# Forget rows in two buffers and masked in place, the last queries earlier, three blocks of the last unit on VectorE

## Chip, cores and metric

The kernel runs on one core of a Trainium2 chip. The metric is the device time of one execution in microseconds (us). The engines are TensorE (PE in the profile, with its weight loads as PEld), VectorE (DVE), ScalarE (ACT), GpSimd (POOL) and SyncE (SP), which here only issues DMA transfers. Every engine works through its own instructions in order. The order on each engine is fixed when the kernel is built: a scheduler takes the instructions as they are written, estimates when each would be ready, and lays out each engine's list; some stretches are pinned to the written order.

## Reference, cut to what matters

One decoder block with two parallel branches over 512 positions and width 1024, in fp32. After an RMS norm one wide projection gives the inputs of both branches.

```python
hN = _rmsnorm(x, norm_g[l])
p = _split_in(hN @ w_in[l])
mq = silu(_causal_dwconv(p["m_q"], ...)); mk = silu(_causal_dwconv(p["m_k"], ...))
mh = _mlstm(mq, mk, p["m_v"], p["m_i"] + b_igate, p["m_f"] + b_fgate)      # 4 heads of 256
mh = _head_layernorm(mh, mh_norm_g[l])
ya = sigmoid(p["m_o"]) * mh * silu(p["m_z"])
yn = _nsa(q_raw, q_rope, kc, vc, ks, vs, kw, vw, gates)                    # 8 heads of 64
yb = yn * silu(p["n_z"])
merged = sigmoid(p["g_a"]) * (ya @ w_branch_a[l]) + sigmoid(p["g_b"]) * (yb @ w_branch_b[l])
x = x + merged @ w_out[l]
return _rmsnorm(x, final_norm_g)
```

In `_mlstm` the scores of a head, q times k, are multiplied by a decay matrix: the exponential of a term of the column position (the input gate minus the running sum of the log forget gate) minus a running maximum, which is a term of the row position, and zero where the column lies after the row. In `_nsa` each query head attends to compressed, selected and windowed keys; the queries of the last two are rotated by position (`_partial_rope`), and each branch's softmax is weighted by a gate.

## The kernel before, in words

All matrices stand as pairs of a rounded high part and the rest (`hTh`/`hTl`, `wh`/`wl` and so on). A product takes three matmuls: high times high, high times low, low times high. The high part is usually made by ACT and the low part by DVE (`split`).

**Start.** `x` comes in four blocks of 128 rows. For each block the mean square is formed on ACT (`square`), a first guess of the reciprocal root by a logarithm and an exponential (`guess`), one Newton step (`newton`, on DVE for blocks 0 and 1, on POOL for 2 and 3; operands of one element per partition), the scaling on DVE (`scaled`), four transposes on PE (`turned`) and the split into `hTh` and `hTl`. In this stretch the engines keep the written order. Meanwhile the small projection's weights are split by POOL, ACT and DVE (`small_hi`, `small_lo`).

**Stream.** The large projection is cut into jobs of 128 columns: a 512 KB weight load on SP (`wr`), the split, 24 matmuls into a PSUM bank of the `pp` ring (L217, L219, L221), and a `post` that reads the bank. Jobs stand in a queue, `stream`, whose loads run two jobs ahead; `stream.step(n)` issues n matmuls of it between other work. The kinds used here:

- `conv_job`: a channel group of the convolution for q or k of the mLSTM branch; its `post` takes an ACT activation, three multiply-adds on DVE, a tanh on ACT, one more DVE product, a split, and a 512 KB store (`qk`).
- `gate_job`: a tanh on ACT and a store (`away`).
- `queries(c)`: two query heads. `rope_a` copies the bank (`rw`), multiplies by the cosines (`ra`), splits the unrotated queries (`rh`, `rl`) and, when the next job begins, moves rows of the copy into `rot` by four small DMAs. `query_heads(c)` multiplies `rot` by the sines, adds, and splits into two `Th` tiles.
- `zpath(c)`: put at the head of the queue when a pair of heads is done.

The queue's order is written by hand: after `queries(1)` come conv, gate, conv, `queries(2)`, conv, gate, conv, gate, conv, `queries(3)`, and then gates and convs in turn.

**Attention units.** 16 units (pair of heads c, head hh, branch b) run in order, with stream matmuls between. While unit i is transposed and multiplied with the values, the scores of unit i + 1 are formed: four row blocks of 128, 256, 384 and 512 columns, each with a fused mask and minimum on DVE, and an exponential on ACT that also gives the row sum. After the fourth one reciprocal of the sums is taken (`st`), and POOL multiplies each block by reciprocal and gate (`P<-P,st,gates`). `ptrans` then transposes four to one blocks on PE into a bank of the `pt` ring (L1020), the result is split into `pth` and `ptl`, and after a lag of three steps multiplied with the values (L1032, L1033). During the units `chores` start copies and sums of weight blocks in DRAM (`wsumv`, `wsumz`, `wsumout`, 1 MB each, issued by SP and POOL).

**Value and gate projections** follow as strips of fewer, summed products, on the same stream. Then the pool `ml` is opened for the **mLSTM heads**. Its tiles have one buffer each unless stated. `fetch_qk(h)` loads q and k of head h (four transfers of 512 KB) and the head's row of running maxima, broadcast to 128 partitions (`gb`, 256 KB, L1376), from DRAM (`decayed`). Four conv jobs run, and more are queued as filler. `decay(h)` makes `Dm`, the decay matrix of head h, in four column blocks of 512, 384, 256 and 128 columns: DVE adds a mask to a copy of the row (`dg`), and ACT takes the exponential of the masked copy for the diagonal 128 columns of each block and of the unmasked `gb` for the rest, seven activations. The head's loop then forms score blocks in two `ps` banks (L170 to L172), DVE multiplies each by its block of `Dm`, in place, and it is split into `Sh` and `Sl`; the value products follow (`num`), their norm (`va`, a power on POOL, some small DVE operations), the products with the gate, `decay(h + 1)`, 30 stream matmuls, and eight transposes (L1510). The output stage ends the kernel.

Of the kernel before, what the change touches and what calls it, by code (L numbers as in the profile page):

```python
# [11 lines left out]
F32 = mybir.dt.float32  # L12
F32R = mybir.dt.float32r
I32 = mybir.dt.int32
AF = mybir.ActivationFunctionType
OP = mybir.AluOpType
AX = mybir.AxisListType.X

T = 512
D = 1024  # L20
NT = T // 128
# [56 lines left out]
def build(  # L78
# [3 lines left out]
    nc = tc.nc  # L82
    ordered = {"act", "dve"}

    class Engine:
# [15 lines left out]
    act, dve, pool = (  # L101
        Engine(e, n) for e, n in ((nc.scalar, "act"), (nc.vector, "dve"), (nc.gpsimd, "pool"))
    )
    A = act.activation
# [170 lines left out]
    gates = pers.tile([128, NT, 24], F32, name="gates")  # L275
    cs = pers.tile([128, NT, 6], F32, name="cs")[:, :, :4]
# [23 lines left out]
    with tc.tile_pool(name="ph0", bufs=2, side="right") as p0, tc.tile_pool(  # L300
        name="small", bufs=1, side="right"
# [16 lines left out]
        bias = sp.tile([128, 32], F32, name="bias")  # L318
# [43 lines left out]
        def newton(tb, e):  # L362
            r, v = rs[tb], vs[tb]
            if e is dve:
                e.scalar_tensor_tensor(v, r, v[:, 0:1], r, OP.mult, OP.mult)
            else:
                e.tensor_tensor(v, r, v, OP.mult)
                e.tensor_tensor(v, r, v, OP.mult)
            e.tensor_scalar(v, v, -0.5, 1.5, OP.mult, OP.add)
            e.tensor_tensor(r, r, v, OP.mult)  # L370

        gp = sp.tile([128, NT, 32], F32, name="gp")
        cols(NKC, lambda ps: blocks(0)(ps))
# [63 lines left out]
        for k in range(7):  # L437
            o = k % 4 * 128
# [139 lines left out]
    def gate_job(n=1):  # L578
        for _ in range(n):
            gate_ab(*gate_jobs.popleft())  # L580
# [25 lines left out]
    def conv_job(n=1):  # L606
        for _ in range(n):
            conv(*conv_jobs.popleft())
# [139 lines left out]
    def queries(c):  # L748
        def post(ps):
            rope_a(ps, ("q", c))  # L750

        cols(NQ + c * 128, post)
# [37 lines left out]
    queries(1)  # L790
    for n in (1, 2, 3):
        conv_job()
        gate_job()
        if n == 1:
            conv_job()
            queries(2)
        elif n == 3:
            conv_job()
            queries(3)
    for _ in range(3):  # L800
        gate_job()
        conv_job()
# [22 lines left out]
    decayed = dram.tile([4, T], F32, name="decayed")  # L825
# [105 lines left out]
    KOFF = [0, 512, 896, 1152]  # L931
# [58 lines left out]
    def score(c, hh, b, qb, pair):  # L990
        kh, kl = KK[c // 2]
        n = (qb + 1) * 128
        tq = heads[c][2][hh][:, qb * 128 : qb * 128 + 128]
        if qb == 0:
            if b == 0:
                pss = PS()
                pe.matmul(pss[:, :256], tq, kh[:, :, :128], start=True, stop=False)
                pe.matmul(pss[:, :256], tq, kl[:, :, :128], start=False, stop=True)
                for i in range(2):
                    softmax_block(c, hh, i, 0, pss[:, i * 128 : i * 128 + 128], *pair[i])  # L1000
            return
        pss = PS()
        pe.matmul(pss[:, :n], tq, kh[:, b, :n], start=True, stop=False)
        pe.matmul(pss[:, :n], tq, kl[:, b, :n], start=False, stop=True)  # L1004
        P, st = pair[b]
        softmax_block(c, hh, b, qb, pss[:, :n], P, st)
        if qb == NT - 1:
            dve.reciprocal(st[:, 2], st[:, 1])
            for j in range(NT):
                pj = P[:, POFF[j] : POFF[j] + (j + 1) * 128]  # L1010
                g = (2 * c + hh) * 3 + 1 + b
                pool.tensor_scalar(
                    pj, pj, st[:, 2, j : j + 1], gates[:, j, g : g + 1], OP.mult, OP.mult
                )

    def ptrans(P, kb):
        n = 512 - kb * 128
# [125 lines left out]
    st = stp.__enter__()  # L1143
# [221 lines left out]
    mp = mlp.__enter__()  # L1365
    cvp.append(mp)
    tiles_of = {}

    def fetch_qk(h):
        for i in range(2):  # L1370
            both = [mp.tile([128, 2, T], F32R, name=f"qk{i}{n}", tag=f"qk{i}{n}") for n in range(2)]
            for n in range(2):
                nc.sync.dma_start(f(both[n]), qk[i, h][:, n])
            tiles_of[i, h] = both
        tiles_of["g", h] = mp.tile([128, T], F32, name="gb", tag="gb")
        nc.sync.dma_start(tiles_of["g", h], decayed[h].partition_broadcast(128))  # L1376

    fetch_qk(0)
    wbv = w_branch_b[0].rearrange("(k p) c -> p k c", p=128)

# [49 lines left out]
    first_of_a(1, PP)  # L1430
    first_of_a(4, PP)

    decays = {}

    def decay(h):
        pgb = tiles_of.pop(("g", h))
        dg = mp.tile([128, T], F32, name="dg", tag="dg")
        dve.tensor_tensor(
            dg.rearrange("p (b t) -> p b t", b=NT), pgb.rearrange("p (b t) -> p b t", b=NT),
            later_only, OP.add,  # L1440
        )
        Dm = mp.tile([128, 1280], F32, name="Dm", tag="Dm")
        for sb in range(NT):
            o, n = KOFF[sb], 512 - sb * 128
            bias = cs[:, sb, h : h + 1]
            A(Dm[:, o : o + 128], dg[:, sb * 128 : sb * 128 + 128], AF.Exp, bias=bias, scale=-1.0)
            if n > 128:
                A(Dm[:, o + 128 : o + n], pgb[:, (sb + 1) * 128 :], AF.Exp, bias=bias, scale=-1.0)
        decays[h] = Dm

    decay(0)
    for h in range(4):
        (qh, ql), (kh, kl) = tiles_of[0, h], tiles_of[1, h]
        vh, vl = vals(h), vals_low(h)
        Dm = decays.pop(h)
        Sh = mp.tile([128, 1280], F32R, name="Sh", tag="Sh")
        Sl = mp.tile([128, 1280], F32R, name="Sl", tag="Sl")
        for sb in range(NT):
            o, n = KOFF[sb], 512 - sb * 128
            pss = PS()  # L1460
            ss = slice(sb * 128, sb * 128 + 128)
            mm3(
                pss[:, :n], lambda k: kh[:, k, ss], lambda k: kl[:, k, ss],
                lambda k: qh[:, k, sb * 128 :], lambda k: ql[:, k, sb * 128 :], range(2),
            )
            dv = Dm[:, o : o + n]
            dve.scalar_tensor_tensor(dv, pss[:, :n], 0.015625, dv, OP.mult, OP.mult)
            split(dv, Sh[:, o : o + n], Sl[:, o : o + n])
            stream.step(6)
        if h < 3:  # L1470
            fetch_qk(h + 1)
        chores.popleft()()
        num = mp.tile([128, NT, 258], F32, name="num", tag="num")
        bs = mp.tile([128, NT, 6], F32, name="bs", tag="bs")
        mv = mp.tile([128, NT, 2], F32, name="mv", tag="mv")
        for tb in range(NT):
            po = PT()
            for sb in range(tb + 1):
                a = KOFF[sb] + (tb - sb) * 128
                lh, ll = Sh[:, a : a + 128], Sl[:, a : a + 128]  # L1480
                pe.matmul(po[:, :258], lh, vh[:, sb, :], start=sb == 0, stop=False)
                pe.matmul(po[:, :256], lh, vl[:, sb, :], start=False, stop=False)
                pe.matmul(po[:, :258], ll, vh[:, sb, :], start=False, stop=sb == tb)
            A(num[:, tb], po[:, :258], AF.Copy)
            dve.bn_stats(bs[:, tb], num[:, tb, 0:256])
            dve.bn_aggr(mv[:, tb], bs[:, tb])
            stream.step(6)
        rho = mp.tile([128, NT], F32, name="rho", tag="rho")
        va = mp.tile([128, NT], F32, name="va", tag="va")
        A(rho, num[:, :, 256], AF.Abs)  # L1490
        dve.tensor_tensor(rho, rho, em[:, :, h], OP.max)
        dve.reciprocal(rho, rho)
        dve.tensor_tensor(va, rho, rho, OP.mult)
        dve.tensor_tensor(va, va, mv[:, :, 1], OP.mult)
        dve.tensor_scalar(va, va, EPS, None, OP.add)
        r = rsqrt(mp, va, NT, "rl")
        dve.tensor_tensor(rho, rho, r, OP.mult)
        nb = mp.tile([128, NT], F32, name="nb", tag="nb")
        dve.scalar_tensor_tensor(nb, mv[:, :, 0], -1.0, rho, OP.mult, OP.mult)
        for tb in range(NT):  # L1500
            nt = num[:, tb, 0:256]
            A(nt, nt, AF.Identity, bias=nb[:, tb : tb + 1], scale=rho[:, tb : tb + 1])
            dve.tensor_tensor(nt, nt, gate[:, tb, h * 256 : h * 256 + 256], OP.mult)
        if h < 3:
            decay(h + 1)
        stream.step(NORM_FILL)
        for e in range(2):
            pt = PT()
            for tb in range(NT):
                pe.transpose(  # L1510
                    pt[:, tb * 128 : tb * 128 + 128], num[:, tb, e * 128 : e * 128 + 128], ident
                )
            ct = h * 2 + e
            gain = prm[:, ct, 10:11]
            A(ya(ct), pt, AF.Copy, scale=gain)
            dve.scalar_tensor_tensor(yal[:, ct], pt, gain, f(ya(ct)), OP.mult, OP.subtract)
            stream.step(6)
# [308 lines left out]
```

## Time and profile before

| | us |
|---|---|
| median of 3 runs (lowest, highest) | 614.73 (611.95, 616.93) |
| profiled execution, its own time | 614.69 |
| profiled execution, its span | 612.9 |
| PE busy | 594.9 |
| DVE busy | 457.9 |
| ACT busy | 357.5 |
| POOL busy | 117.6 |

The mean granted TensorE clock of the profiled execution is 0.993. In the profile's rows a line of the kernel, an engine and an operation are followed by the tiles written and read; L93 is the helper through which all DVE, ACT and POOL operations pass, so these are told apart by their tiles. A row of the timeline gives start, length, engine, line, operation, tiles and shape, the number of merged operations, and in brackets how long the engine stood idle before it and what it had waited for. A row of a stretch gives the busy time and count of PE, PEld, DVE, ACT and POOL, the granted clock, the busy share of the DMA engines and GB/s. The start of the kernel runs to about 27 us, the attention units from about 80 to 275, the strips to about 390, the mLSTM heads to about 535, and the output stage to the end.

### The profile page before, as it was taken

The page shows a single profiled execution, that of the slowest core. Times are in us where ns is not written, and L with a number is a line of the kernel's source. Part 1 is how long each engine was busy: PE and PEld are TensorE (multiplying, and loading weights), DVE is VectorE, ACT ScalarE, POOL GpSimd, SP SyncE. Part 2 cuts the span into 40 slices and gives each one's busy share as a digit, 9 for nine tenths or more (in the row PEclk, how much of TensorE's full clock was granted, in tenths as well). Part 3 has the DMA queues.
Part 4 walks back from the last instruction along what each step waited for, and adds up shares of the span by engine and source line. Part 5 has one row for each costly group of instructions (what it writes and reads, how often), then busy time and mean ns, then how long its engine had stood idle before and what let it go on. Part 6 is the DMA issues. An engine that isn't in the chain of part 4 may idle for free.

```text
span 612.9 us, 8649 instructions
## 1 busy us (share of the span) xinstructions
PE 594.9 (97%) x2927; PEld 494.4 (81%) x2927; DVE 457.9 (75%) x864; ACT 357.5 (58%) x669; POOL 117.6 (19%) x197
## 2 busy tenths in 40 slices
PE   7999999999999999999999999998999999999995
PEld 5988888888887888878888888887887888878884
DVE  4767769898687878659979655678676675579984
ACT  5675656666576566556756565565665632444554
POOL 6322107334124532330000000000200010001114
PEclk9999999999999999999999999998999999999998
DMA  8759867967936886588675456799897686398733
GB/s 286 220 155 259 233 206 139 244 137 231 306 104 138 183 183 196 176 154 244 222 240 170 153 183 204 211 295 294 245 284 235 203 198 217 123 335 284 244 113 137
DMA packets 105302, 128.48 MB, mean 210 GB/s; under 512 B 6165, under 2 KB 66709, under 8 KB 105130
## 3 DMA queue, kind: packets, MB, share of 16 engines
q1 hardware_dynamic: 98632, 111.93, 58.6%
q0 software_dynamic: 6048, 14.95, 13.6%
q10 hardware_dynamic: 578, 1.05, 0.5%
q8 instruction: 23, 0.38, 0.2%
q14 instruction: 21, 0.17, 0.1%
HBM read 109.61 MB, written 42.02 MB: 247 GB/s over the span
## 4 chain that ended last, share of the span: by engine, by line
PE 45%; DVE 3%; DMA 3%; ACT 2%; issue 1%; POOL 0%; SPq 0%; POOLq 0%; ACTq 0%
DMA gb<-decayed 3%; PE pp L221 3%; PE pp L219 3%; PE pp L217 3%; PE pp L1248 3%; PE pp L1250 3%; PE pp L1252 3%; PE pt L1250 2%; PE pt L1252 2%; PE pt L1248 2%; PE pp L1567 2%; PE pp L1571 2%; PE pp L1569 2%; PE ps L1248 1%; PE ps L1250 1%; PE ps L1252 1%
## 5 line engine op out<-in xcount | busy, mean ns | idle before, releaser
L93 DVE TENSOR_TENSOR wl<-wr,wh 128x1024 fp32r<-128x1024 f32 (+2 forms) x105 | 126.6, 1208 | 46.7 <-ACT wh L93 46.2
L93 ACT ACTIVATE wh<-wr 128x1024 fp32r<-128x1024 f32 (+2 forms) x105 | 108.3, 1033 | 60.5 <-PE pp L219 10.9
L217 PE MATMUL pp<-hTh,wh 128*128 128x512 f32 x352 | 140.4, 399 | 0.0
L219 PE MATMUL pp<-hTl,wh 128*128 128x512 f32 x352 | 140.3, 399 | 0.0
L221 PE MATMUL pp<-hTh,wl 128*128 128x512 f32 x352 | 139.9, 398 | 0.0
L93 POOL TENSOR_SCALAR P<-P,st,gates 128x128 f32<-128x128 f32 (+1 forms) x64 | 51.3, 837 | 138.3 <-DVE st L93 77.8
L221 PEld LDWEIGHTS pp<-hTh,wl 128*128 128x128 f32 x352 | 66.6, 189 | 11.8
L219 PEld LDWEIGHTS pp<-hTl,wh 128*128 128x128 f32 x352 | 66.8, 190 | 11.1
L217 PEld LDWEIGHTS pp<-hTh,wh 128*128 128x128 f32 x352 | 66.8, 190 | 11.1
L93 ACT ACTIVATE P<-P,st 128x128 f32<-128x128 f32 (+3 forms) x64 | 35.6, 557 | 34.0 <-DVE st L93 33.6
L93 POOL TENSOR_TENSOR rlr<-va,mhalf 128x4 f32<-128x4 f32 x4 | 4.1, 1033 | 236.3 <-DVE va L93 236.3
L93 DVE CUSTOM_DVE_ANT_0 P<-ps,cst 128x128 f32<-128x128 f32 (+3 forms) x64 | 30.2, 483 | 12.8 <-PE ps L1004 10.8
L93 ACT ACTIVATE pth<-pt 128x512 fp32r<-128x512 f32 (+1 forms) x64 | 26.7, 433 | 20.9 <-PE pt L1020 14.9
L93 DVE TENSOR_TENSOR ptl<-pt,pth 128x512 fp32r<-128x512 f32 (+1 forms) x64 | 30.4, 482 | 9.3 <-ACT pth L93 9.0
L93 DVE SCALAR_TENSOR_TENSOR u<-pp,prm,u 128x511 f32<-128x511 f32 (+2 forms) x48 | 35.6, 741 | 0.9 <-ACT u L93 0.6
L1020 PE MATMUL pt<-cst,P 128*128 128x128 f32 x160 | 29.0, 278 | 2.9 <-DVE ptl L93 1.8
L1020 PEld LDWEIGHTS pt<-cst,P 128*128 128x128 f32 x160 | 20.3, 141 | 13.6 <-DVE ptl L93 6.4
L93 ACT ACTIVATE th<-u 128x512 f32<-128x512 f32 x16 | 10.1, 630 | 20.8 <-DVE u L93 19.4
L1033 PE MATMUL po<-ptl,vsw 128*128 128x512 f32 (+1 forms) x64 | 21.3, 334 | 0.0
L1032 PE MATMUL po<-pth,vsw 128*128 128x512 f32 (+1 forms) x64 | 20.7, 324 | 0.3 <-ACT pth L93 0.3
L1250 PE MATMUL pp<-wl,S 128*128 128x512 f32 x48 | 18.7, 390 | 0.0
L1252 PE MATMUL pp<-wh,S 128*128 128x512 f32 x48 | 18.7, 390 | 0.0
(389 smaller groups left out, 1353.0 us busy)
## 6 DMA issues: line engine op xcount, KB each, us to landing
wr<-w_in SPq DMA_DIRECT2D x68, 512.0 KB
qk<-hl SPq DMA_DIRECT2D x16, 512.0 KB
qk<-qk SPq DMA_DIRECT2D x16, 512.0 KB
wsumv<-w_in SPq DMA_DIRECT2D x4, 1024.0 KB
away<-s SPq DMA_DIRECT2D x16, 256.0 KB
wsumz<-w_in SPq DMA_DIRECT2D x4, 1024.0 KB
wsumout<-w_out SPq DMA_DIRECT2D x4, 1024.0 KB
wr<-wsumv SPq DMA_DIRECT2D x8, 512.0 KB
```

What stands on the lines that cost most here:

```text
L93: ins = fn(*args, **kw)
L217: pe.matmul(ps, a, c, start=k == 0, stop=False)
L219: pe.matmul(ps, a, d, start=False, stop=False)
L221: pe.matmul(ps, b, c, start=False, stop=k == nk - 1)
L1020: pe.transpose(pt[:, (qb - kb) * 128 : (qb - kb) * 128 + 128], P[:, POFF[qb] + kb * 128 : POFF[qb] + kb * 128 + 128], ident,)
L1032: pe.matmul(po[:, kb * 128 :], vl, th[:, :n], start=b == 0 and kb == 0, stop=False)
L1033: pe.matmul(po[:, kb * 128 :], vl, tl[:, :n], start=False, stop=False)
L1248: pe.matmul(ps, a, c, start=begin, stop=False, skip_group_check=not first)
L1250: pe.matmul(ps, a, d, start=False, stop=False, skip_group_check=not first)
L1252: pe.matmul(ps, b, c, start=False, stop=k == 3, skip_group_check=not first)
L1567: pe.matmul(ps, p, ya(k), start=k == 0, stop=False)
L1569: pe.matmul(ps, p, yal[:, k], start=False, stop=False)
```

## The change

Four parts.

1. `decay` and its row: `gb` gets two buffers and is fetched by a function of its own, `fetch_decay`. Rows 0 and 1 are fetched ahead of q and k of head 0, row h + 2 behind q and k of head h + 1. The tile `dg` goes; the three exponentials of the unmasked columns come first, then the mask is added to the row in place, then the four exponentials of the diagonal blocks.
2. `queries(3)` is queued ahead of the last gate job and conv job that stood before it.
3. The first three row blocks of the last unit (128, 256 and 384 columns) are scaled by DVE, the fourth by POOL.
4. The Newton step on DVE uses tensor-scalar forms, with the second factor as a scalar of each partition.

```diff
@@ newton @@
             if e is dve:
-                e.scalar_tensor_tensor(v, r, v[:, 0:1], r, OP.mult, OP.mult)
+                e.tensor_scalar(v, v, r[:, 0:1], r[:, 0:1], OP.mult, OP.mult)
...
-            e.tensor_tensor(r, r, v, OP.mult)
+            if e is dve:
+                e.tensor_scalar(r, r, v[:, 0:1], None, OP.mult)
+            else:
+                e.tensor_tensor(r, r, v, OP.mult)
@@ the queue @@
     for n in (1, 2, 3):
         conv_job()
+        if n == 3:
+            queries(3)
         gate_job()
         if n == 1:
             conv_job()
             queries(2)
         elif n == 3:
             conv_job()
-            queries(3)
@@ score @@
-                pool.tensor_scalar(
-                    pj, pj, st[:, 2, j : j + 1], gates[:, j, g : g + 1], OP.mult, OP.mult
-                )
+                e = dve if (c, hh, b) == units[-1] and j < 3 else pool
+                e.tensor_scalar(pj, pj, st[:, 2, j : j + 1], gates[:, j, g : g + 1], OP.mult, OP.mult)
@@ fetch_qk @@
-        tiles_of["g", h] = mp.tile([128, T], F32, name="gb", tag="gb")
-        nc.sync.dma_start(tiles_of["g", h], decayed[h].partition_broadcast(128))
-
+
+    decays = {}
+
+    def fetch_decay(h):
+        decays["g", h] = mp.tile([128, T], F32, name="gb", tag="gb", bufs=2)
+        nc.sync.dma_start(decays["g", h], decayed[h].partition_broadcast(128))
+
+    fetch_decay(0)
+    fetch_decay(1)
     fetch_qk(0)
@@ decay @@
     def decay(h):
-        pgb = tiles_of.pop(("g", h))
-        dg = mp.tile([128, T], F32, name="dg", tag="dg")
-        dve.tensor_tensor(
-            dg.rearrange("p (b t) -> p b t", b=NT), pgb.rearrange("p (b t) -> p b t", b=NT),
-            later_only, OP.add,
-        )
+        gb = decays.pop(("g", h))
         Dm = mp.tile([128, 1280], F32, name="Dm", tag="Dm")
+        cols_of = lambda sb: (KOFF[sb], 512 - sb * 128, cs[:, sb, h : h + 1])
+        for sb in range(NT - 1):
+            o, n, bias = cols_of(sb)
+            A(Dm[:, o + 128 : o + n], gb[:, (sb + 1) * 128 :], AF.Exp, bias=bias, scale=-1.0)
+        blocks_ = gb.rearrange("p (b t) -> p b t", b=NT)
+        dve.tensor_tensor(blocks_, blocks_, later_only, OP.add)
         for sb in range(NT):
-            ...
+            o, n, bias = cols_of(sb)
+            A(Dm[:, o : o + 128], gb[:, sb * 128 : sb * 128 + 128], AF.Exp, bias=bias, scale=-1.0)
@@ heads @@
         if h < 3:
             fetch_qk(h + 1)
+            if h < 2:
+                fetch_decay(h + 2)
```

More of the change, by code (lines that the diff above doesn't have):

```diff
@@ L1431, in build @@
     first_of_a(4, PP)
-    decays = {}
     def decay(h):
-        pgb = tiles_of.pop(("g", h))
-        dg = mp.tile([128, T], F32, name="dg", tag="dg")
-        dve.tensor_tensor(
-            dg.rearrange("p (b t) -> p b t", b=NT), pgb.rearrange("p (b t) -> p b t", b=NT),
-            later_only, OP.add,
-        )
-        Dm = mp.tile([128, 1280], F32, name="Dm", tag="Dm")
-        for sb in range(NT):
[L1444 to L1448, printed above, removed]
+        gb = decays.pop(("g", h))
+        Dm = mp.tile([128, 1280], F32, name="Dm", tag="Dm")
+        cols_of = lambda sb: (KOFF[sb], 512 - sb * 128, cs[:, sb, h : h + 1])
[4 more added lines that the diff above has]
+        dve.tensor_tensor(blocks_, blocks_, later_only, OP.add)
+        for sb in range(NT):
+            o, n, bias = cols_of(sb)
+            A(Dm[:, o : o + 128], gb[:, sb * 128 : sb * 128 + 128], AF.Exp, bias=bias, scale=-1.0)
         decays[h] = Dm
```

## Prediction

> **What bounds the kernel now.** I read the page's busy times and slices first, then the same in stretches, then what TensorE waited for.
>
> ```profile
> span 612.9 us, 8649 instructions
> PE 594.9 (97%) x2927; PEld 494.4 (81%) x2927; DVE 457.9 (75%) x864; ACT 357.5 (58%) x669; POOL 117.6 (19%) x197
> ...
> PEclk9999999999999999999999999998999999999998
> ...
> 420.00:440.00 20.00, 17.88 (x89) 15.26 (x89) 14.13 (x37) 11.15 (x25) 3.38 (x3) 0.91 0.88 279
> ...
> 423.40:426.80 3.40, 3.40 (x11) 2.79 (x10) 2.04 (x5) 2.37 (x5) 0.00 (x0) 0.50 1.03 325
> ```
>
> TensorE (PE) is the bound: 594.9 of 612.9 us. Almost everywhere its queue is full, so an edit on another engine gains only what it takes out of PE's few holes, and what the holes cost afterwards. One is in 420 to 440, and behind it the granted clock falls to 0.50 for 3.4 us. Half a clock for 3.4 us is 1.7 us lost. The edits can reach these holes:
>
> ```profile
> 14.09 0.63 PE L405 MATMUL pt<-cst,xt 128*128 128x128 f32 x4 [1.04 <-issue]
> 197.88 0.44 PE L1020 MATMUL pt<-cst,P 128*128 128x128 f32 x2 [1.10 <-DVE ptl L93]
> 268.69 0.41 PE L1020 MATMUL pt<-cst,P 128*128 128x128 f32 x2
> 269.69 0.33 PE L1020 MATMUL pt<-cst,P 128*128 128x128 f32 x1 [0.59 <-POOL P L93]
> 270.52 0.48 PE L219 MATMUL pp<-hTl,wh 128*128 128x512 f32 x1
> 419.79 0.39 PE L217 MATMUL pp<-hTh,wh 128*128 128x512 f32 x1
> 422.30 0.33 PE L170 MATMUL ps<-qk,qk 128*128 128x128 f32 x1 [2.12 <-DVE Dm L93]
> 470.14 0.39 PE L219 MATMUL pp<-hTl,wh 128*128 128x512 f32 x1
> 470.36 0.39 PE L221 MATMUL pp<-hTh,wl 128*128 128x512 f32 x1
> 471.26 1.00 PE L1510 MATMUL pt<-cst,num 128*128 128x128 f32 x3 [0.52 <-DVE num L93]
> 472.44 0.48 PE L217 MATMUL pp<-hTh,wh 128*128 128x512 f32 x1
> ...
> 441.85 0.44 PE pt L1510 x4
> ```
>
> I count start to start, since ends are modelled: a 512-column matmul normally starts 0.23 us after the one before (470.14 to 470.36), and four transposes take 0.44 us (the chain's piece at 441.85). So the hole at 420 is 422.30 - 419.79 - 0.23 = 2.28 us; at 470 it is (471.26 - 470.36 - 0.23) + (472.44 - 471.26 - 0.44) = 1.41; the last unit's four transposes lose 270.52 - 268.69 - 0.44 = 1.39. With 1.7 for the clock this is 6.8 us; the two others follow.
>
> **The forget rows.** The chain of waits and VectorE's (DVE) timeline show why DVE is late at 422.30:
>
> ```profile
> 394.65 9.38 DMA gb<-decayed
> 410.42 4.53 DMA gb<-decayed
> 458.81 5.60 DMA gb<-decayed
> ...
> 404.06 0.69 DVE L93 TENSOR_TENSOR dg<-gb,cst 128x512 f32<-128x512 f32 x1 [2.01 <-DMA gb<-decayed]
> 414.97 0.69 DVE L93 TENSOR_TENSOR dg<-gb,cst 128x512 f32<-128x512 f32 x1 [0.88 <-DMA gb<-decayed]
> 464.43 0.69 DVE L93 TENSOR_TENSOR dg<-gb,cst 128x512 f32<-128x512 f32 x1 [2.83 <-DMA gb<-decayed]
> 400.69 0.63 ACT L93 ACTIVATE th<-u 128x512 f32<-128x512 f32 x1 [2.92 <-DVE u L93]
> ```
>
> Head 0's row stands behind four 512 KB loads of q and k and lands 9.38 us after issue. Head 1's can be issued only when ACT has read the single buffer (410.42). Each time the mask add `dg` is at the head of DVE's in-order queue and holds convolution and score work behind it: 2.01, 0.88 and 2.83 us. After 414.97 DVE has no idle until the `Dm` product that frees the score bank PE waits for. The change takes from this queue, ahead of 422: 2.01 us of waiting (head 0's row now goes first; at the 4.5 to 5.6 us of the other two it lands near 398, against a mask that stood ready at 402), 0.88 of waiting, and head 1's add itself, 0.69, because that add now follows three exponentials into `Dm`, which head 0 holds until its last score block. That is 3.58 us against a hole of 2.28. PE's pace caps the early part, so some of it will not arrive; I take 2.0 of the 2.28 (bounds 0 and 2.28). The half clock came 1.1 us after an idle of 2.12, while the idles of 1.04 and 1.10 above are followed by no such slice (the page's clock digit falls to 8 only in the slice around 420 and at the very end), so with at most some 0.3 us left the 1.7 goes too: **3.7 us**, bounds 0 and 4.0. At 470, DVE loses 2.83 of waiting and 0.69 of add ahead of the `num` products, more than the 1.41 hole: I take **1.3**, bounds 0 and 1.4.
>
> Costs. The SyncE (SP) queue: q and k of head 0 stand behind two row fetches, 0.5 MB; at the 279 GB/s of the row 420 to 440 that is 1.9 us. In the trace they landed before 404.03, when the row issued behind them was in; first use is the score matmul at 412.39, so 6 us are free. Weight loads behind move by one fetch, 0.9 us; the one issued at 395.66 was first read at 411.12 by an ACT that did not wait for it. The fetches of rows 2 and 3 now follow q and k of heads 1 and 2 (423.82, 453.32), when their buffer has long been read, so SP no longer stands on a buffer. In `decay` the arithmetic is the same (seven exponentials, one 0.69 add); the order is new, and the add waits for ACT. The first three exponentials of head 0 (0.60, 0.50, 0.39 us in the timeline) fit in the 2.92 us in which ACT waited before 400.69.
>
> **The start.** Two small DVE operations change form:
>
> ```profile
> 11.77 2.79 POOL L93 TENSOR_TENSOR slo<-sraw,shi 128x576 fp32r<-128x576 f32 x2
> 11.84 0.15 DVE L93 TENSOR_SCALAR v<-v 128x1 f32<-128x1 f32 x1
> 12.03 1.18 DVE L93 TENSOR_TENSOR r<-r,v 128x1 f32<-128x1 f32 x1
> 12.35 0.69 PE L430 MATMUL pp<-shi,hTl 128*128 128x288 f32 x4
> ```
>
> One element per partition takes 1.18 us with two tensor inputs beside a GpSimd (POOL) operation, and 0.15 as a tensor-scalar in the same stretch. PE runs dry near 12.9 (four matmuls of 0.13 after 12.35) and gets the scaled rows at 14.09: 1.2 us, all behind this 1.18. Written as tensor-scalar the operation saves 1.0, the other form change some 0.3. The work up to 27 us is chained to it, but the second to fourth row blocks go through POOL and ACT. I take **0.9**, bounds 0.4 and 1.2.
>
> **The last unit.** POOL scales four blocks one after the other, and the transposes wait for the third (269.69 above) and the fourth:
>
> ```profile
> 267.05 3.34 POOL L93 TENSOR_SCALAR P<-P,st,gates 128x128 f32<-128x128 f32 x4 [7.93 <-PE pt L1020]
> 266.75 0.53 DVE L93 TENSOR_TENSOR ptl<-pt,pth 128x384 fp32r<-128x384 f32 x1
> 267.92 0.42 PE L1033 MATMUL po<-ptl,vsw 128*128 128x384 f32 x1
> L93 POOL TENSOR_SCALAR P<-P,st,gates 128x512 f32<-128x512 f32 x16 | 20.3, 1268 | 0.0
> ...
> 27.14 0.19 DVE L93 TENSOR_SCALAR kk<-kk 128x64 f32<-128x64 f32 x1
> ```
>
> With only the 512-column block POOL ends near 267.05 + 1.27 = 268.3, ahead of 268.69. DVE's tensor-scalar is shown at 1 and 64 columns (0.15 and 0.19); along that line 128 + 256 + 384 columns cost 3 x 0.15 + 768 x 0.0006 = 0.9 us; the bounds are 0.45 (three of one column) and 1.25 (the two-input `ptl` forms, 0.28, 0.42 and 0.55). They stand at the reciprocal and push the `ptl` splits of the unit before back by as much; the 384-column one ended 0.64 ahead of its matmul at 267.92, so PE pays at most 0.3 to 0.6. Net **0.8** of 1.39, bounds -0.5 and 1.4.
>
> [...]
>
> **The last queries.** They move ahead of one gate job and one convolution; work is only reordered.
>
> ```profile
> 157.04 0.57 ACT L93 ACTIVATE s<-pp 128x512 f32<-128x512 f32 x1
> 184.36 0.58 ACT L93 ACTIVATE rw<-pp 128x512 f32<-128x512 f32 x1
> 191.19 0.69 DVE L93 TENSOR_TENSOR rot<-rot,St 128x512 f32<-128x512 f32 x1 [1.57 <-DMA rot<-rw]
> 157.64 0.61 SPq L869 DMA_DIRECT2D wsumz<-w_in  x1
> 166.00:171.00 5.00, 4.80 (x26) 3.76 (x26) 5.00 (x12) 1.66 (x6) 0.00 (x0) 1.00 0.95 272
> ```
>
> Now the rotated copy is written at 184.36, its four small DMAs hold DVE 1.57 us at 191.19, and PE's hole at 197.88 (1.27 start to start) follows. After, the copy comes where the gate's tanh is now, 157.04; its four issues on SP (184.96 to 187.7, 2.8 us) then stand ahead of the gate's store, a weight sum and the next weight load, which have until the next job, 8 us later; and 2.8 us of DVE work move out of 191 to 200 into 160 to 180. The hole may go, but a similar wait can appear at the new place: **0.4**, bounds -8 (below) and 1.3.
>
> **The sum.** 3.7 + 1.3 + 0.9 + 0.8 + 0.4 = 7.1 us. The profiled execution took 614.69 (span 612.9 and 1.8 around it), the median of the runs is 614.73, so nothing is to be converted: **607.6 us**, 1.2% less.
>
> **Rivals.** First, the wait only changes its name: DVE now stands on ACT instead of the DMA. ACT spreads its seven `Dm` exponentials among other work:
>
> ```profile
> 454.75 0.60 ACT L93 ACTIVATE Dm<-gb,cs 128x384 f32<-128x384 f32 x1
> 458.38 0.40 ACT L93 ACTIVATE Dm<-gb,cs 128x128 f32<-128x128 f32 x1
> ```
>
> From the first to the end of the third of the unmasked ones are 4.0 us. An add queued too early would hold DVE as long as the DMA did, for head 3 the 1.3 (608.9), and for the first heads the 3.7 with the clock (612.6). Against it: these adds have 15 us and more before their `Dm` is used. Chance 0.22. Second, VectorE and POOL block each other in the last unit: one POOL block of 1.27 is added to DVE, the 0.8 becomes -0.5: 608.9; chance 0.13. Third, the slower side: the rotated copy's DMAs fall behind two 1 MB weight sums issued from 157.64, with the DMA engines busy until 171 (a share of 0.95 in the row 166 to 171). The multiply stood 5.3 us behind its copy now (191.19 - 1.57 - 184.36), so about 162.3 after; landing at 171 it holds DVE 8.7 us, PE (0.3 of slack, as in 1.57 against 1.27) 8.4, and the clock 1.7 more. Against 6.7 left of the gain this ends at 618. It decides from a hold of about 5.3 us. Chance 0.07. Fourth, the reordered queues also close small holes elsewhere in 100 to 260: 604.5; chance 0.08. The forecast keeps 0.50, its own spread 605.6 to 609.5.
>
> One per cent of 614.7 is 6.1 us, about what a measurement of this kernel can tell from no change; the border is 608.6. The forecast lies three quarters below it, the fourth rival wholly, the second and first nearly not: faster 0.48, slower by over 1% (above 620.9) 0.03, within 0.49. The range 605.0 to 612.6 reaches to the first rival's end and leaves out the third and half of the fourth.
>
> **What would show it.** No DVE idle on `gb`, no PE idle over 0.5 us on `Dm` and no half clock between 400 and 440; the transposes at 470 starting without idle; PE at 14 us about 1 us earlier; the last unit's four transposes in under 0.9 us; DVE waiting under 2 us for `rot`. I am wrong if an idle over 2 us appears on the mask add, on `rot`, or behind the last unit's blocks, with the clock behind it.

## The result, and the profile after

The changed kernel took 607.1 us (median of 6 runs, 606.62 to 607.74), the kernel before 614.26 beside it (6 runs, 611.69 to 616.93): a ratio of 0.9885, 95% interval 0.9853 to 0.9916. The forecast was 607.6. The profiled execution took 607.15 with a span of 605.3, 7.6 us less than before. The page of the changed kernel (span, busy times, granted clock in 40 slices):

```profile
span 605.3 us, 8654 instructions
PE 592.5 (98%) x2927; PEld 493.7 (82%) x2927; DVE 456.4 (75%) x867; ACT 359.0 (59%) x669; POOL 113.7 (19%) x194
...
PEclk9999999999999999999999999999999999999998
```

The digit 8 around 420 us is gone from the clock; only that of the very end is left. Next the stretches that hold the holes of the first two heads, and what PE waited for (total, times, longest; one more wait has 0.3):

```profile
420.00:440.00 20.00, 20.00 (x107) 17.05 (x106) 16.06 (x39) 12.86 (x27) 3.38 (x3) 1.00 1.04 276
440.00:480.00 40.00, 40.00 (x214) 34.52 (x213) 29.32 (x63) 24.60 (x50) 1.04 (x1) 1.00 0.68 215
...
PE ps L325 <- POOL epst L93: 2.8, 1, 2.8
PE pt L1023 <- DVE ptl L93: 0.8, 2, 0.5
PE pp L1574 <- ACT wh L93: 0.5, 1, 0.5
```

Where 17.88 of 20 us were busy between 420 and 440, it is now 20.00, and `Dm`, `num` and POOL's `P` no longer stand among the waits. (The 2.8 us at the very start are common to both.) Where the time was gained is read by following the same matmul through both kernels. Before, then after: the first projection job, the first strip, the first score blocks of heads 0, 1 and 2, the last matmul.

```profile
27.14 0.40 PE L217 MATMUL pp<-hTh,wh 128*128 128x512 f32 x1
275.95 0.39 PE L1248 MATMUL ps<-wh,hTh 128*128 128x512 f32 x1
412.39 0.39 PE L170 MATMUL ps<-qk,qk 128*128 128x512 f32 x1
445.36 0.39 PE L170 MATMUL ps<-qk,qk 128*128 128x512 f32 x1
475.74 0.40 PE L170 MATMUL ps<-qk,qk 128*128 128x512 f32 x1
605.12 0.28 PE L1690 MATMUL pp<-T4h,mx 128*128 128x256 f32 x1
...
26.85 0.40 PE L217 MATMUL pp<-hTh,wh 128*128 128x512 f32 x1
272.46 0.39 PE L1251 MATMUL ps<-wh,hTh 128*128 128x512 f32 x1
409.47 0.39 PE L170 MATMUL ps<-qk,qk 128*128 128x512 f32 x1
438.34 0.39 PE L170 MATMUL ps<-qk,qk 128*128 128x512 f32 x1
467.23 0.39 PE L170 MATMUL ps<-qk,qk 128*128 128x512 f32 x1
596.98 0.28 PE L1697 MATMUL pp<-T4h,mx 128*128 128x256 f32 x1
```

| stretch | lead at its end, us | gained in it | forecast |
|---|---|---|---|
| start | 0.29 | 0.29 | 0.9 |
| stream and units | 3.49 | 3.20 | 0.4 + 0.8 |
| strips | 2.92 | -0.57 | 0 |
| head 0 | 7.02 | 4.10 | 3.7 |
| head 1 | 8.51 | 1.49 | 1.3 |
| rest | 8.14 | -0.37 | 0 |

Within the second row the trace puts 1.43 us ahead of unit 10 (the last queries) and 1.77 at the last unit. The span shrank by 0.5 less than the last lead, since 8.3 us follow the last matmul and not 7.8. The rows at the changed places:

```profile
11.83 0.21 DVE L93 TENSOR_SCALAR r<-r,v 128x1 f32<-128x1 f32 x1
167.23 0.69 DVE L93 TENSOR_TENSOR rot<-rot,St 128x512 f32<-128x512 f32 x1
173.02 0.44 PE L1023 MATMUL pt<-cst,P 128*128 128x128 f32 x2 [0.46 <-DVE ptl L93]
267.78 0.95 PE L1023 MATMUL pt<-cst,P 128*128 128x128 f32 x7
394.03 1.28 ACT L93 ACT_TABLE_LOAD   x1 [4.57 <-DMA gb<-decayed]
399.89 0.68 DVE L93 TENSOR_TENSOR gb<-gb,cst 128x512 f32<-128x512 f32 x1
```

The Newton product takes 0.21 instead of 1.18 us; `rot` and the mask add carry no wait; the last unit's transposes run on without one. New is a small hole at 173, behind the moved queries; the one at 197.88 is gone.

### The profile page after: what moved, and what is told of

Read it like the earlier page. It is cut to its first block, busy times and chain, and to the rows that moved or that the text cites. A ratio compares the mean times of both kernels' runs of the same rounds, so it can differ in the third digit from the quotient of the medians.

```text
span 605.3 us, 8654 instructions
## 1 busy us (share of the span) xinstructions
PE 592.5 (98%) x2927; PEld 493.7 (82%) x2927; DVE 456.4 (75%) x867; ACT 359.0 (59%) x669; POOL 113.7 (19%) x194
## 4 chain that ended last, share of the span: by engine, by line
PE 88%; DVE 6%; ACT 3%; issue 1%; DMA 1%; POOL 1%; POOLq 0%; ACTq 0%; DVEq 0%
PE pp L217 13%; PE pp L219 13%; PE pp L221 13%; PE pt L1023 3%; PE pp L1251 2%; PE pp L1253 2%; PE pp L1255 2%; DVE wl L93 2%; PE pp L433 2%; PE pp L1574 2%; PE pp L1578 2%; PE pp L1576 2%; PE po L1036 1%; ACT wh L93 1%; PE po L1035 1%; PE pt L1255 1%
## 5 line engine op out<-in xcount | busy, mean ns | idle before, releaser
L93 POOL TENSOR_SCALAR P<-P,st,gates 128x512 f32<-128x512 f32 (+3 forms) x61 | 47.3, 812 | 138.5 <-DVE st L93 89.6
L1253 PE MATMUL pt<-wl,S 128*128 128x512 f32 x48 | 18.7, 389 | 0.0
```

The lines of the kernel that those rows point to most:

```text
L93: ins = fn(*args, **kw)
L1253: pe.matmul(ps, a, d, start=False, stop=False, skip_group_check=not first)
```

## The experiments

The theory: VectorE's in-order list was late at two places of the heads, the first hole pulled the clock down, and the three other parts each close one hole. Against it stand: the gain is all of one part; fetching early or masking in another order is what pays; the clock falls for another cause than the hole. Holes are counted start to start, as in the forecast. Ten variants and the changed kernel itself ran in three groups, each beside the kernel before, which measured 613.94, 614.0 and 613.96 us. Ranges are lowest to highest, and ratios are to the kernel before with a 95% interval.

**The rows alone** (`e1_rows`: part 1 on the kernel before, that is the hunks of `fetch_qk`, `decay` and `heads` shown with the change).

> The forget rows alone (two buffers, fetched ahead, masked in place), on the kernel before. Theory (the waits of the mask add made the hole at 420 us, and the hole made the clock fall): no PE idle over 0.5 us between 400 and 440, no stretch of half clock there, transposes at 470 without idle, 5.4 us less than before: about 609. Rival (the half clock there has another cause): the hole goes, but a half-clock stretch of 3.4 us stays somewhere between 400 and 440: about 610.7. Rival (the gain of the whole change lies in the other parts): within 1 us of before.

609.68 us (609.34 to 611.11), ratio 0.9915 (0.9883 to 0.9946). In its profile head 0 gains 4.09 and head 1 1.5 us, as in the whole change, and the half clock is absent:

```profile
420.00:440.00 20.00, 20.00 (x110) 17.21 (x109) 15.53 (x40) 14.22 (x30) 3.38 (x3) 1.00 1.04 307
```

So the largest part is worth 4.3 of the 7 us.

**The last queries alone** (`e2_queries`).

```diff
         conv_job()
+        if n == 3:
+            queries(3)
         gate_job()
...
-            queries(3)
```

> The earlier last queries alone, on the kernel before. Theory (the wait of the rot multiply on its DMAs made the hole at 198 us): DVE does not wait on rot, the hole of 1.27 us is under 0.3, unit 10 begins 1.2 to 1.5 us earlier, the rest is as before: about 613. Rival (the hole comes from ScalarE's chain of exponentials and splits): the hole stays near 1 us and unit 10 begins within 0.4 us of before.

612.65 us (609.12 to 614.91), ratio 0.9968 (0.9938 to 0.9998): 1.3 us. The profile shows 1.44 gained ahead of unit 10; the hole at 197 is down from 1.27 to 0.2, one of 0.63 stands at 173 (the transposes that wait for `ptl`), and head 0's is as it was.

**The last unit alone** (`e3_unit`).

```diff
-                pool.tensor_scalar(
-                    pj, pj, st[:, 2, j : j + 1], gates[:, j, g : g + 1], OP.mult, OP.mult
-                )
+                e = dve if (c, hh, b) == units[-1] and j < 3 else pool
+                e.tensor_scalar(pj, pj, st[:, 2, j : j + 1], gates[:, j, g : g + 1], OP.mult, OP.mult)
```

> Three blocks of the last unit on VectorE alone, on the kernel before. Theory: the four last transposes lose nothing on POOL, the ptl splits of unit 14 run up to 0.9 us later, the strips begin 1 to 1.8 us earlier, and the strips' splits, which come out in another order on VectorE, give back 0.6 near 317: 613.2. Rival (VectorE and GpSimd hold each other): VectorE's first block lasts until POOL's block is done (0.7 us and more, where 128 columns alone should take 0.25) and the strips begin within 0.5 us of before.

612.18 us (610.67 to 615.23), ratio 0.9974 (0.9948 to 1.0). Its profile held two surprises, in the start and in head 0:

```profile
11.77 0.33 DVE L93 TENSOR_TENSOR r<-r,v 128x1 f32<-128x1 f32 x1
12.06 1.42 POOL L93 TENSOR_TENSOR slo<-sraw,shi 128x576 fp32r<-128x576 f32 x1
...
420.69 0.33 PE L170 MATMUL ps<-qk,qk 128*128 128x128 f32 x1 [2.14 <-DVE Dm L93]
416.56:419.97 3.41, 1.99 (x11) 1.36 (x9) 3.41 (x6) 0.66 (x2) 0.00 (x0) 1.00 1.09 378
419.97:423.38 3.41, 2.69 (x16) 2.43 (x17) 2.89 (x8) 2.13 (x5) 0.00 (x0) 1.00 0.99 299
423.38:426.80 3.42, 3.42 (x20) 2.95 (x20) 2.90 (x6) 3.42 (x10) 0.00 (x0) 1.00 1.05 280
```

The unchanged two-input product took 0.33 here instead of 1.18, and POOL's split happened to begin 0.3 us later than in the profile of before (12.06 against 11.77), behind it and not ahead. And the hole of 2.1 us was there, but no half clock followed it. More on both below. The last unit did as the theory says: VectorE's first block lasted 0.70, as in the rival, but the strips began 2.66 us earlier, 1.07 of it from the start.

This profile also gives the price of the half clock. From the fourth score block to the first transposes of `num`, TensorE runs the same 96 matmuls without idle in the profile of before and here (before, then `e3_unit`):

```profile
441.69 0.60 PE L1510 MATMUL pt<-cst,num 128*128 128x128 f32 x4
438.52 0.92 PE L1509 MATMUL pt<-cst,num 128*128 128x128 f32 x4
```

Before, they take 441.69 - 422.30 = 19.39 us, here 438.52 - 420.69 = 17.83. `e2_queries` and `e4_newton`, which have the hole and the half clock, take 19.41 and 19.40. So the half clock cost about 1.6 us.

**The Newton step alone** (`e4_newton`).

```diff
-                e.scalar_tensor_tensor(v, r, v[:, 0:1], r, OP.mult, OP.mult)
+                e.tensor_scalar(v, v, r[:, 0:1], r[:, 0:1], OP.mult, OP.mult)
...
-            e.tensor_tensor(r, r, v, OP.mult)
+            if e is dve:
+                e.tensor_scalar(r, r, v[:, 0:1], None, OP.mult)
+            else:
+                e.tensor_tensor(r, r, v, OP.mult)
```

> The tensor-scalar forms of the Newton step alone, on the kernel before. Both theories: the 1.18 us operation takes about 0.2. Theory (what was gained there is given back by the start of the clock): the first projection job begins 1.2 us earlier when the full clock starts near 10.4 us as in the profile of before, and 0.3 us earlier when it starts near 12.5 as in the profile of after. Rival (the operation holds nothing up): it begins at 27.1 as before, whenever the clock starts. The time alone, at most 1.2 us less, will not tell them apart.

613.17 us (611.77 to 617.84), ratio 0.9985 (0.9956 to 1.0014): no difference shown. The first job starts 1.16 earlier, with the clock full at 10.0 us, as the theory says; 0.6 of it is lost again where the hole at 195 grows from 1.27 to 1.93, since the last queries were still late there.

**Fetch or order?** `e5_row0` changes only the fetch (one buffer, row ahead of its q and k), `e6_order` only the order of masking:

```diff
e5_row0, on the kernel before, in fetch_qk
+        tiles_of["g", h] = mp.tile([128, T], F32, name="gb", tag="gb")
+        nc.sync.dma_start(tiles_of["g", h], decayed[h].partition_broadcast(128))
         for i in range(2):
...
-        tiles_of["g", h] = mp.tile([128, T], F32, name="gb", tag="gb")
-        nc.sync.dma_start(tiles_of["g", h], decayed[h].partition_broadcast(128))
e6_order: fetch_qk as before; decay as in the change
```

> The kernel before, with one thing changed: each head's forget row is issued ahead of that head's q and k instead of behind them; one buffer, the separate masked copy and the order of the exponentials stay. If head 0's late row is the first cause of the hole at 420, VectorE loses its 2.01 us wait near 404, keeps head 1's 0.88 wait and 0.69 add near 414, and the hole falls from 2.28 to 0.3 to 0.9 us with no half clock behind it; the hole at 470 stays. Then 610.3 to 611.5 us against 613.9. If the place of head 1's add makes the hole, it stays over 1.5 us and the time is 613 to 614.

> The kernel before, with the rows fetched as before (one buffer, behind q and k), but masked in place: exponentials of the unmasked blocks, then the mask add, then the diagonal blocks. Head 0's row still lands near 404, now in front of ScalarE's queue. If late rows are the cause, VectorE still waits (now on the exponentials, 1 to 2 us near 405), while head 1's add leaves the stretch ahead of 422: the hole at 420 falls only to about 0.7 to 1.5 us, the one at 470 by at most half, and the time is 611 to 613. If the order alone gives the gain, both holes go and the time is 609.5 to 610, as with the rows part alone (609.68).

`e5_row0`: 611.45 us (609.9 to 613.14), ratio 0.9953 (0.993 to 0.9977). `e6_order`: 609.17 us (607.97 to 610.39), ratio 0.9914 (0.989 to 0.9938), the whole of what part 1 brings. First and last of the four mask adds of `e5_row0` on VectorE and a wait of its PE, then 440 to 480 in `e6_order` and its first mask add:

```profile
395.85 0.69 DVE L93 TENSOR_TENSOR dg<-gb,cst 128x512 f32<-128x512 f32 x1 [2.65 <-DMA gb<-decayed]
460.39 0.69 DVE L93 TENSOR_TENSOR dg<-gb,cst 128x512 f32<-128x512 f32 x1 [3.31 <-DMA gb<-decayed]
467.22 1.00 PE L1510 MATMUL pt<-cst,num 128*128 128x128 f32 x3 [0.98 <-DVE num L93]
...
440.00:480.00 40.00, 40.00 (x211) 34.39 (x210) 31.57 (x65) 23.40 (x44) 1.04 (x1) 1.00 0.76 238
407.53 0.68 DVE L93 TENSOR_TENSOR gb<-gb,cst 128x512 f32<-128x512 f32 x1
```

The early fetch moves head 0's wait to 395, and head 1's add, which still waits 1.31, from 414.97 to 407.38; head 0's hole falls to 0.19. But the last add still stands on its row at the head of VectorE's list, and `num` is late at 467. The order closes both holes. Counted in VectorE's list of 864 instructions, the four adds were the 569th, 581st, 625th and 656th before and are the 574th, 605th, 646th and 694th in `e6_order`: the add follows exponentials into `Dm`, so it is laid out behind the work it used to hold up, and none waits for a row, though head 0's is issued no earlier than before (395.63 against 394.65). My expectation for `e6_order`, that VectorE would wait for the exponentials, was wrong.

The new lists differ in one more thing, which the forecast did not have. The fourth score block stands on the bank that head 0's second `Dm` product frees. On VectorE, before, then after:

```profile
416.85 0.68 DVE L93 SCALAR_TENSOR_TENSOR Dm<-ps,Dm 128x512 f32<-128x512 f32 x1
419.95 1.22 DVE L93 TENSOR_TENSOR wl<-wr,wh 128x1024 fp32r<-128x1024 f32 x1
421.69 0.88 DVE L93 SCALAR_TENSOR_TENSOR Dm<-ps,Dm 128x384 f32<-128x384 f32 x2
...
412.94 0.68 DVE L93 SCALAR_TENSOR_TENSOR Dm<-ps,Dm 128x512 f32<-128x512 f32 x1
416.06 0.88 DVE L93 SCALAR_TENSOR_TENSOR Dm<-ps,Dm 128x384 f32<-128x384 f32 x2
```

Before, six operations stand between the two products, a weight split (`wl`) of 1.22 us among them, and the second comes 4.84 us behind the first. After, it comes 3.12 behind, with four operations between and the split later in the list; so it is in `e1_rows` and `e5_row0`, and in `e6_order` it comes 1.25 behind with one. The first product came 4.46 us behind head 0's first score matmul before and 3.47 after (3.97 in `e5_row0`, 3.47 in `e6_order`). So against the scores the second product gained 2.7 us: 1.0 from what stood ahead of the first one, the waits and the add, and 1.7 from the new order behind it. No run has the one without the other.

**The hole filled** (`e7_filled`): idle replaced by work of no use.

```diff
+            if h == 0 and sb == 3:
+                spare = PO()
+                for _ in range(9):
+                    pin(pe.matmul(spare, hTh[:, 0, 0:128], hTh[:, 0, :], start=True, stop=True))
```

> The kernel before with nine 512-column matmuls whose result is not used (9 x 0.227 = 2.04 us) in TensorE's queue right ahead of head 0's fourth score block, that is in the hole at 420; VectorE's and ScalarE's work is as before. If the idle makes the clock fall, the hole is now filled with work, there is no slice at half clock behind it, the fourth score block starts where it did, and the time is 0 to 1.7 us below before (612.2 to 613.9), with head 0 to head 1 about 1.7 us shorter than in the profile of before. If the clock falls for another reason (work on the other engines, the place in the program), a half clock of 3.4 us follows near 423 all the same and the time is 613.9 to 614.5.

618.06 us (616.37 to 619.01, and one of 739.05), ratio 1.0068 (1.0045 to 1.0091): slower, against both expectations. At the place itself the theory's picture is there; the loss comes 20 us later. PE's row of the fillers and the stretch behind them, then VectorE's mask add of head 2, and two windows of 3.4 us around the `num` transposes:

```profile
420.42 2.20 PE L1463 MATMUL po<-hTh 128*128 128x512 f32 x9
423.22:426.64 3.42, 3.42 (x21) 2.96 (x21) 1.87 (x5) 2.01 (x5) 0.00 (x0) 1.00 1.04 336
...
437.67 0.69 DVE L93 TENSOR_TENSOR dg<-gb,cst 128x512 f32<-128x512 f32 x1 [3.21 <-DMA gb<-decayed]
440.29:443.70 3.41, 1.21 (x6) 0.55 (x4) 1.98 (x9) 1.64 (x4) 2.76 (x3) 1.00 0.90 169
443.70:447.11 3.41, 3.38 (x9) 2.31 (x10) 2.82 (x5) 2.62 (x4) 0.00 (x0) 0.50 0.93 133
```

The hole at 420 was full of work and the clock stayed at 1.00. But the lists came out otherwise, head 2's mask add stood 3.21 us on its row ahead of the norm's small operations, PE was idle for 2.2 us before the transposes, and there the half clock followed. So the same fault came out at another place; as a measure of the clock's price in time the run is inconclusive, and that price stands on `e3_unit` above.

**Three variants of the changed kernel, and itself again** (`e11_again`, no edit).

```diff
e8_two, on the changed kernel
-                e = dve if (c, hh, b) == units[-1] and j < 3 else pool
+                e = dve if (c, hh, b) == units[-1] and j < 2 else pool
e9_nofetch, on the changed kernel (fetch_decay and its calls go)
             tiles_of[i, h] = both
+        decays["g", h] = mp.tile([128, T], F32, name="gb", tag="gb")
+        nc.sync.dma_start(decays["g", h], decayed[h].partition_broadcast(128))
e10_nounit, on the changed kernel
-                e = dve if (c, hh, b) == units[-1] and j < 3 else pool
+                e = pool
```

> The changed kernel with two blocks of the last unit (128 and 256 columns) on VectorE instead of three; GpSimd takes the 384- and the 512-column one. VectorE's blocks then hold its splits back by about 1.0 us instead of 1.41, and the strips behind keep the order that they had before. Theory: the hole of 0.66 us at 317 goes and the last unit loses no more than now, 0.3 to 0.9 us off: 606.2 to 606.8 against 607.1. Rival: GpSimd's two blocks (0.7 and 0.76 us one after the other) become late for the last unit's transposes, 0.4 us or more lost there: 607.1 to 607.6.

> The changed kernel without its fetching two heads ahead: one buffer for the forget rows, each issued behind its head's q and k as before; the masking in place and its order, and the three other parts, stay. If the order of masking alone gives the rows' part of the gain (as 609.17 against 609.68 for the whole part says), nothing changes: 606.6 to 607.7, no hole over 0.5 us between 400 and 480 and no half clock. If the early rows are needed once the other parts move the work earlier, VectorE waits for the three exponentials near 402, the hole before head 0's fourth score block comes back with 0.5 to 2 us, and the time is 608 to 611.

> The changed kernel with all four blocks of the last unit on GpSimd again; the three other parts stay. If the last unit's part is worth in this company what its own run gave alone (612.18 against 613.94, with some 1 us of it from the start, so 0.8), the transposes of the last unit lose 1.2 to 1.4 us again and the time is 607.7 to 608.4. If the strips behind give it all back, 607.1 as now; if its full 1.77 us counts, 608.9.

> The changed kernel as it is, beside the three others on the same chip: 606.6 to 607.7 as before. Its profile shows whether the late clock of the start (full at 12.5 us in its first profile, 9.3 to 10.6 in the seven others) belongs to the change: if it does, it comes at 12 to 13 again and the first projections start 0.3 us earlier than before; if it is chance, it comes near 10 and they start about 1.1 us earlier.

| kernel | median (range), 6 runs | ratio to before, 95% |
|---|---|---|
| `e11_again` | 606.03 (605.41 to 607.19) | 0.9867 (0.983 to 0.9903) |
| `e8_two` | 606.31 (605.76 to 609.37) | 0.9879 (0.9839 to 0.9918) |
| `e9_nofetch` | 606.82 (605.71 to 607.67) | 0.9873 (0.9832 to 0.9913) |
| `e10_nounit` | 607.24 (606.71 to 608.55) | 0.9887 (0.985 to 0.9924) |

Without the early fetch the time is the same within its spread: from the first job to head 2, 7.90 us are gained against 7.75 with it. The last unit is worth 1.2 us in this company; without it PE stands twice on POOL again (0.60 and 0.42 us). Two blocks on VectorE instead of three bring no measurable gain. The groups of these blocks on VectorE (shortest, median, longest in ns), in the changed kernel and in `e8_two`, say why, and a late window of the profile of `e8_two`, which is its slowest run (609.37), explains that one:

```profile
L93 DVE TENSOR_SCALAR P<-P,st,gates x3: 401/471/699, 265.5 to 266.4; 128x128 f32<-128x128 f32 x1, 128x256 f32<-128x256 f32 x1, 128x384 f32<-128x384 f32 x1
L93 DVE TENSOR_SCALAR P<-P,st,gates x2: 592/754/917, 265.3 to 265.8; 128x128 f32<-128x128 f32 x1, 128x256 f32<-128x256 f32 x1
...
540.88:544.29 3.41, 1.75 (x7) 0.81 (x6) 3.41 (x6) 2.67 (x3) 1.21 (x2) 1.00 0.99 276
544.29:547.71 3.42, 3.42 (x10) 2.65 (x9) 3.42 (x7) 2.00 (x3) 0.00 (x0) 0.50 0.77 230
```

Beside one POOL block one of VectorE's ran long (128 columns, 0.70 us), beside two POOL blocks both did (0.59, and 0.92 for the 256 columns that took 0.40 in the changed kernel), so two blocks cost it as much as three: 1.42 us against 1.41. In the profile of `e8_two` PE waited in the output stage for a `wh` (holes of 0.66 and 1.33 us) and a half clock followed; up to head 2 it was level with `e11_again` (leads of 8.80 and 8.82).

## Why the prediction was right, step by step

- **The rows, 3.7 + 1.3.** The profile shows 4.10 and 1.49, the run alone 4.3 in the median. The place and the sum held: no idle of VectorE on `gb`, none of PE on `Dm`, no half clock. The reason was half wrong. I counted 2.01 us of waiting as removed by "head 0's row now goes first". `e5_row0` shows that an earlier row is enough for the first hole alone, but `e6_order` and `e9_nofetch` show that it isn't needed: it is enough that the mask add became dependent on work that comes late, and so lost its early place in VectorE's list. And of the 3.58 us of waits and add that stood ahead of the first `Dm` product, only 1.0 reached it. By that alone the hole of 2.28 would have kept about 1.3 (an estimate, 2.28 - 0.99); the rest came from the list behind that product, where the scheduler set a weight split later. That 2.0 of 2.28 came so near is in part luck.
- **The half clock, 1.7 of the 3.7,** was taken as certain behind a hole of 2.1 us. It isn't: of the four profiles with that hole three had it, and there it cost 1.6. Over the 58 runs of before in the three groups (without one of 2095.13), the 27 with a mean granted clock of 0.996 or more have a median of 612.87 us, the 22 at 0.993 or less 615.71. The six of `e11_again` lie at 0.995 to 0.997. So part of the gain is the clock that no longer falls, and probably part of the narrower spread; but the difference of 2.8 is more than one fall costs, and the mean also holds the fall at the end of the kernel (from 607.7 on in the profile of before), so it doesn't price the clock.
- **The start, 0.9** (bounds 0.4 to 1.2): 0.29 in the first profile, 1.07 in `e11_again`, 0.43 to 0.66 in the other three with the change. The operation saved what was said, 0.97 (1.18 to 0.21). The term rested on one execution of each kind: in `e3_unit` and `e5_row0` the unchanged product took 0.33 and 0.36 and the first job came 1.07 and 1.04 earlier without any edit. And the clock became full at 10.4 us in the profile of before, 12.5 in that of after (10.8 in `e11_again`, but 10.0 in `e4_newton` with the same start, so why it came late stays open). The matmuls of the start ran slow for longer:

```profile
11.52 1.15 PE L433 MATMUL pp<-shi,hTl 128*128 128x288 f32 x4
```

  Before, four of the same took 0.70 from 11.02.
- **The last unit, 0.8**: VectorE's three blocks first held PE back by 0.8 (unit 14 led by 1.73, the first transposes of unit 15 by 268.69 - 267.78 = 0.91; I had allowed 0.3 to 0.6), and then more was gained than the 1.39 of the hole, 1.77 net. Of this the strips gave back 0.57 (0.92 in `e11_again`). Not foreseen: VectorE's blocks also change the order of the strips' weight splits, and near 317 the lead falls from 3.50 to 2.89 within a dozen matmuls; `e8_two`, with the old order of these splits, doesn't have that. By `e10_nounit` the part is worth 1.2 us. The second rival came in part: VectorE's 128 columns took 0.70 beside POOL's block, at a price of about 0.4 (an estimate: 0.40 and 0.47 for 256 and 384 columns point to 0.33 for 128 alone). That such a block costs 1.3, which also gave the 0.8 its lower bound, was the author's estimate and no run shows it: POOL's one block took 0.76 and not the 1.27 of the mean, and was already under way (265.31, VectorE's first 265.46). In `e8_two` 256 columns took 0.92 beside POOL's second block, against 0.40 in the changed kernel, where POOL's only block was done.
- **The last queries, 0.4**: mis-sized, 1.43 in the profile and 1.3 alone. I priced the whole hole of 1.27 at a third, for fear that a wait would open at the new place. It did, with 0.46 at 173, but 0.5 more was gained at 208, in unit 9. The third rival's hold of 8.7 us didn't come: the `rot` product at 167.23 stands on nothing.
- **The first rival** (the wait changes its name) is excluded by the timeline of after; ACT took over 4.57 us of waiting for head 0's row, near 394, at no cost to PE.
- **Given back** in the output stage: 0.37. Of this 0.10 is a hole at `wh` that was there before and grew from 0.44 to 0.55, and 0.30 is lost near 569.5, where TensorE's weight load waits 0.43 for VectorE's `wl`. The forecast had no term for such losses.

The single parts, 4.26 + 1.29 + 1.76 + 0.77, add up to 8.1, the whole to 7.2 and 7.9 in its two groups. (The profile of the 1.76 gained 1.07 at the start without an edit; whether its other runs did isn't shown.) That the total came within 0.5 of the forecast is also luck: by the profile the last unit and the queries gained 2.0 more than forecast and the rows 0.6, while the start fell 0.6 short, the strips and the output stage gave back 0.9, and 0.5 went behind the last matmul.

## What to carry to other kernels

When an engine with an in-order list stands on a transfer, look first at why the waiting instruction lies so early: a dependence that sends it behind the work it holds up can be worth as much as a faster transfer, and costs no buffer. Price a hole on the busiest engine together with what follows it, but take such a price from several executions: the half clock followed three of four holes of about the same length, and the product of the start took 1.18 us begun 0.26 behind POOL's split and 0.33 begun 0.29 ahead of it. After an edit to one engine's list, read the stretches behind it as well, since the scheduler lays other work out anew (0.6 to 0.9 us went there).

## What the runs showed of the hardware

**The half clock lasted 3.41 us.** Wherever the clock fell within a kernel, it stayed at 0.50 for 3.41 us: from 423.39 in the profile of before, 422.91 in `e2_queries`, 423.04 in `e4_newton`, 443.70 in `e7_filled` and 544.29 in `e8_two`. In the 3.41 us ahead of it PE's busy time was 1.21 (`e7_filled`), 1.75 (`e8_two`), and in the first three rows here (before, `e2_queries`, `e4_newton`) 1.29, 1.60 and 1.46:

```profile
419.98:423.39 3.41, 1.29 (x9) 1.05 (x9) 3.41 (x7) 1.54 (x4) 0.00 (x0) 1.00 0.86 279
419.50:422.91 3.41, 1.60 (x10) 1.48 (x11) 3.41 (x8) 1.35 (x3) 0.00 (x0) 1.00 0.89 281
419.63:423.04 3.41, 1.46 (x10) 1.34 (x10) 3.41 (x7) 1.35 (x3) 0.00 (x0) 1.00 1.01 337
...
194.35:197.76 3.41, 1.65 (x9) 1.01 (x7) 3.08 (x5) 3.36 (x7) 0.97 (x3) 1.00 0.57 181
```

The last row (`e4_newton`) with 1.65 had the clock at 1.00 behind it, and so had 1.62 in `e6_order` (194.96 to 198.37). In `e3_unit` the stretches of this length from 416.56 and 419.97, which share its hole, had 1.99 and 2.69, and nothing followed. So PE's busy time in such a stretch does not part these profiles by one value, as 1.75 was followed by a half clock and 1.62 and 1.65 were not; ends are modelled, and what makes the clock fall is not shown. At the end of the kernel it is at half as well, in the profile of before from 607.7 on, behind the last matmuls.

**Which of two engines began first cost 0.85 us here.** The one-element product of the start took 1.18 us in the profile of before, where it began 0.26 behind POOL's split (12.03 and 11.77), and 0.33 in `e3_unit`, where it began 0.29 ahead of it (11.77 and 12.06). With the old form `e1_rows` and `e2_queries` have the first order too, with 1.18 and 1.17 us, and `e5_row0` the second, with 0.36.
